# Grouping 22 mixer tiles as 2 + 6 + 6 + 8 and adding the residual by transfers in a four-layer encoder kernel

## The chip, the cores and the metric

The kernel runs on one core of a Trainium2 chip. A core has a matrix engine (TensorE, PE in the profile, with PEld for its weight loads), VectorE (DVE), ScalarE (ACT) and GpSimd (POOL), and a queue engine SyncE (SP) that here only issues transfers (DMA). Each engine takes its instructions strictly in order from its own list; semaphores hold an instruction until its inputs are there. What counts is the device time of one execution in microseconds (us); less is better.

## The reference, cut to what matters

Four layers work on x of 512 tokens by 1024 channels. Each has a token mixer (convolution, neighbourhood attention, retention, convolution) and then a gated convolutional FFN with 2816 hidden channels, that is 22 tiles of 128. The change is in the FFN alone:

```python
def rmsnorm(x, g):
    y = x * lax.rsqrt(jnp.mean(x * x, axis=-1, keepdims=True) + EPS)
    return y * g

def conv_ffn(h, w_up, dw_w, dw_b, w_down):
    u = dwconv(h @ w_up, dw_w, dw_b)          # width 3 over the tokens
    val, gate = jnp.split(u, 2, axis=-1)
    return (jax.nn.gelu(gate) * val) @ w_down

for i in range(DEPTH):
    ...
    h = rmsnorm(x, norm2_g[i])
    x = x + conv_ffn(h, ffn_w_up[i], ffn_dw_w[i], ffn_dw_b[i], ffn_w_down[i])
```

## The kernel before, in words

x lies in SBUF as eight tiles x[0..7] of 128 channels by 512 tokens, for the whole program. Every float32 operand of a product is split in a high half (a cast on ACT, "hi", "wh", "h") and a low half (source minus high half, on VectorE, "lo", "wl", "l"); mm3 (L170 to 173) makes three matmuls of them: high by high, low by high, high by low.

**FFN, up.** `up(n)` loads one tile of 1024 weights into one of two raw buffers (load_raw), splits it (split_w, L166 and L167; three buffers of each half), and makes 24 matmuls 512 wide on the eight splits of x times the norm's gain. There are 44 ups: even n the value tile n/2, odd n the gate tile. The factor 1/rms is not in these splits: `up_first` runs ups 0 and 1 together and then `stats1`, which sums the squares over channels (L211 on TensorE, L213 on VectorE) and works out rstd_col in twelve small instructions of VectorE (to L267); `stats2` spreads it over the partitions (L218 on TensorE, an ACT copy) into rstd_bc after up S2 = 2 (4 in layer 1). `mid(j)` then takes value and gate tile j: times rstd_bc (L309), the width-3 convolution (one ACT, two VectorE instructions, L312 to 316), gelu, and their product.

**FFN, down.** The 22 mixer tiles are taken as ten pairs and two left over (tiles 20 and 21). A pair is a 2 by 2 block matrix F (two tiles by two halves of the 512 tokens), and so are the weights of a macro i (output tiles 2i and 2i+1, a11, a12, a21, a22). Seven products of sums of blocks (as in Strassen's and Winograd's scheme) replace eight: mid forms the sums of F on GpSimd (L333 to L337) and splits seven blocks into Hh and Hl; `weights(i, q)` brings the raw blocks, forms s1 = a21 + a22 and s3 = a21 + a11 by accumulating transfers on GpSimd's queue (L388, L389), s2 and sg by additions on VectorE, and splits all of them. `prod` makes 3 matmuls 256 wide for each pair of the group.

The pairs come in three groups, PARTS = (0,4), (4,7), (7,10). A group's `down` runs as soon as its mids are done: the first at j = 8, the second at j = 14, the final one after all ups. In a down, each macro i works in two banks of PSUM: xc collects a11, s2, s3; v collects a22 and s1, and later sg and a12. After s2 a copy s12 of xc's states is taken and x[2i+1] is added to it on GpSimd (L464); after s3, ACT takes xc negated (L471), VectorE makes u2 = -xc - v (L473), and GpSimd adds that to x[2i] (L476). The `tail` of a macro (sg and a12 into v, then x[2i+1] = v + s12, L448) is written behind the next macro's s2. In the final group `remainder` does the two left-over tiles 512 wide for each macro, and `after(k)` prepares x[k] for the next stage: casts and low halves (L238, L241) and squares.

**What sets the order.** The code is written in one order, and a list scheduler (schedule_with_timeline_sim, in the kernel function) interleaves it by its own costs, subject to buffers and data; the result is a fixed list for each engine. `tc.issue_after(ins)` keeps an instruction behind another one. The weights of the downs in before have no such gate, so loads and splits for which a buffer is free may be placed far ahead.

## Time and profile before

| | us |
|---|---|
| median of three timed runs (2601.73 to 2607.19) | 2601.84 |
| the profiled execution, its own time | 2609.96 |
| its span in the profile | 2608.2 |
| mean granted TensorE clock of it | 0.99 |

The FFN stages begin at 211.6, 845.4, 1654.6 and 2233.6 us of the trace and last some 380 us each. The page lists busy time by engine, then what waited for what. In a row of waits the columns are: the waiting engine, its tile and line, what it waited for; then total us, times, longest us. In a window's row they are: us of the window, and for each engine the busy us with the number of instructions; then the granted clock of TensorE (1.00 is full speed), the share of the DMA engines and GB/s. In a timeline row: start in us, duration, engine, line, operation, output and inputs with their shapes, and in brackets the idle time before it and what ended it.

### The profile page before, as it was taken

Reading aid. Unit: us, or ns where it says so; the run is one execution under the profiler, and the core shown is the slowest. Engines: PE = TensorE matmul, PEld = TensorE weight load, DVE = VectorE, ACT = ScalarE, POOL = GpSimd, SP = SyncE. Lnnn points to the kernel's source line nnn. Section 1 sums busy time; section 2 is a strip of 40 time slices with the busy share of each in tenths; the row PEclk is TensorE's granted clock in tenths of the full one; section 3 lists DMA queues with packets and bytes.
Section 4 is the critical chain, followed back from the end, with each engine's and each line's share of the span. In section 5 each row is a group of like instructions: output and inputs, shape, how many; then the busy total and the mean of one; then the engine's idle time right before and its main releaser. Section 6 shows DMA issues by size and latency. Waiting matters only on the chain.

```text
span 2608.2 us, 38020 instructions
## 1 busy us (share of the span) xinstructions
PE 2544.1 (98%) x14788; PEld 2176.2 (83%) x14788; DVE 1933.9 (74%) x2980; ACT 1185.0 (45%) x1695; POOL 649.7 (25%) x649
## 2 busy tenths in 40 slices
PE   9999999989999999998999999999999999999998
PEld 7887898879998788887888888789888887789887
DVE  7976867777877887787666565687777787686777
ACT  5454444455556444444332323444444445444443
POOL 1215132234421332313000000313232221223322
PEclk9999999999999999999999999999999999999999
DMA  6726354433233544533222221535343572435443
GB/s 238 229 78 192 97 137 110 117 89 99 86 92 93 135 112 118 134 86 97 89 73 73 86 76 65 142 94 138 93 130 100 169 224 80 138 95 138 108 121 86
DMA packets 110006, 303.53 MB, mean 116 GB/s; under 512 B 14033, under 2 KB 37201, under 8 KB 109825
## 3 DMA queue, kind: packets, MB, share of 16 engines
q1 hardware_dynamic: 89136, 266.82, 33.5%
q0 software_dynamic: 19392, 31.56, 6.9%
q10 hardware_dynamic: 1296, 2.72, 0.3%
q8 instruction: 116, 1.90, 0.3%
q14 instruction: 66, 0.53, 0.1%
HBM read 291.64 MB, written 5.63 MB: 114 GB/s over the span
## 4 chain that ended last, share of the span: by engine, by line
PE 72%; DVE 9%; DMA 5%; issue 2%; ACT 2%; POOL 1%; DVEq 0%; SPq 0%; POOLq 0%; ACTq 0%
PE ps L171 20%; PE ps L173 20%; PE ps L172 20%; DVE wl L167 3%; PE ps L176 3%; PE ps L178 3%; PE ps L177 3%; DMA wt<-in_f_down 3%; DMA wr<-in_f_down 2%; ACT wh L166 1%; DVE t L314 1%; DVE t L316 1%; DVE Hl L345 1%; DVE xl L241 1%; PE ps L628 1%
## 5 line engine op out<-in xcount | busy, mean ns | idle before, releaser
L171 PE MATMUL ps<-xh,wh 128*128 128x512 f32 x1856 | 740.5, 400 | 1.2 <-ACT wh L166 1.2
L173 PE MATMUL ps<-xh,wl 128*128 128x512 f32 x1856 | 735.3, 397 | 0.1
L172 PE MATMUL ps<-xl,wh 128*128 128x512 f32 x1856 | 735.2, 396 | 0.0
L166 ACT CAST wh<-wr 128x1024 fp32r<-128x1024 f32 (+1 forms) x362 | 372.7, 1030 | 656.4 <-PE ps L172 429.3
L167 DVE TENSOR_TENSOR wl<-wr,wh 128x1024 fp32r<-128x1024 f32 (+1 forms) x359 | 448.9, 1251 | 132.4 <-ACT wh L166 131.8
L173 PEld LDWEIGHTS ps<-xh,wl 128*128 128x128 f32 x1856 | 350.4, 189 | 85.9 <-DVE wl L167 0.5
L171 PEld LDWEIGHTS ps<-xh,wh 128*128 128x128 f32 x1856 | 350.8, 189 | 83.7 <-ACT wh L166 2.8
L172 PEld LDWEIGHTS ps<-xl,wh 128*128 128x128 f32 x1856 | 350.7, 189 | 82.9 <-DVE xl L241 0.4
L173 PE MATMUL ps<-Hh,wl 128*128 128x256 f32 x640 | 176.7, 285 | 10.6 <-DVE wl L167 10.6
L172 PE MATMUL ps<-Hl,wh 128*128 128x256 f32 x640 | 180.4, 284 | 2.1 <-DVE Hl L345 1.5
L171 PE MATMUL ps<-Hh,wh 128*128 128x256 f32 x640 | 178.0, 284 | 0.4 <-ACT wh L166 0.4
L312 ACT ACTIVATE t<-t,par 128x512 f32<-128x512 f32 x176 | 141.7, 813 | 57.7 <-DVE t L309 57.0
L176 PE MATMUL ps<-wh,xh 128*128 128x256 f32 (+1 forms) x512 | 159.1, 314 | 0.4 <-ACT qk L763 0.4
L177 PE MATMUL ps<-wl,xh 128*128 128x256 f32 (+1 forms) x512 | 159.3, 312 | 0.0
L178 PE MATMUL ps<-wh,xl 128*128 128x256 f32 (+1 forms) x512 | 159.1, 312 | 0.0
L309 DVE TENSOR_TENSOR t<-ps,rstd_bc 128x512 f32<-128x512 f32 x176 | 119.4, 686 | 51.0 <-PE ps L173 49.0
L171 PE MATMUL ps<-Hh,h 128*128 128x256 f32 x480 | 139.4, 291 | 16.2 <-DVE t L473 12.3
L316 DVE SCALAR_TENSOR_TENSOR t<-t,par,t 128x511 f32<-128x511 f32 x176 | 141.3, 807 | 3.6
L314 DVE SCALAR_TENSOR_TENSOR t<-t,par,t 128x511 f32<-128x511 f32 x176 | 138.9, 794 | 0.0
L172 PE MATMUL ps<-Hl,h 128*128 128x256 f32 x480 | 138.5, 289 | 0.0
L173 PE MATMUL ps<-Hh,l 128*128 128x256 f32 x480 | 138.4, 288 | 0.0
L259 POOL TENSOR_TENSOR sqacc<-t,sqacc 128x512 f32<-128x512 f32 x49 | 75.5, 1541 | 245.4 <-ACT t L254 244.9
(297 smaller groups left out, 5301.3 us busy)
## 6 DMA issues: line engine op xcount, KB each, us to landing
wr<-in_f_up SPq DMA_DIRECT2D x176, 512.0 KB, 3.7
wraw<-in_cdw SPq DMA_DIRECT2D x56, 608.0 KB, 4.8
wr<-in_cw_in SPq DMA_DIRECT2D x30, 512.0 KB, 4.2
wr<-in_f_down SPq DMA_DIRECT2D x32, 384.0 KB, 3.2
wr<-in_nat_qkv SPq DMA_DIRECT2D x24, 512.0 KB, 3.8
wr<-in_cw_out SPq DMA_DIRECT2D x16, 512.0 KB, 4.0
wr<-in_f_down SPq DMA_DIRECT2D x16, 512.0 KB, 3.6
wr<-in_ret_qk SPq DMA_DIRECT2D x16, 512.0 KB, 3.7
```

Of the source, the lines that this page charges most:

```text
L166: nc.scalar.copy(hi[:, :n], raw[:, :n])
L167: eng.tensor_tensor(lo[:, :n], raw[:, :n], hi[:, :n].bitcast(F32), SUB)
L171: nc.tensor.matmul(o, wh, ah, start=first, stop=False, skip_group_check=free)
L172: nc.tensor.matmul(o, wh, al, start=False, stop=False, skip_group_check=free)
L173: nc.tensor.matmul(o, wl, ah, start=False, stop=last, skip_group_check=free)
L176: nc.tensor.matmul(o, ah, wh, start=first, stop=False)
L177: nc.tensor.matmul(o, ah, wl, start=False, stop=False)
L178: nc.tensor.matmul(o, al, wh, start=False, stop=last)
L309: nc.vector.tensor_tensor(u, ps, rstd_bc, MUL)
L312: nc.scalar.activation(a, u, AF.Identity, bias=pc("fdb", l * 44 + c), scale=pt[:, w + 1:w + 2])
L314: nc.vector.scalar_tensor_tensor(a[:, 1:], u[:, :T - 1], pt[:, w:w + 1], a[:, 1:], MUL, ADD)
L316: nc.vector.scalar_tensor_tensor(a[:, :T - 1], u[:, 1:], pt[:, w + 2:w + 3], a[:, :T - 1], MUL, ADD)
```

## The change

- The left-over tiles are now 0 and 1 (REST = 2), and the pairs come in groups of 3, 3 and 4: PARTS = (0,3), (3,6), (6,10), which are 6, 6 and 8 tiles. The downs still run at j = 8, 14 and at the end. The last pair of a group enters its first macro apart (`part`), after the others.
- The left-over products run once, before the final down, from an input f_rest of their own; each of the eight results is copied by ACT and added to x[k] by an accumulating transfer.
- The sums of F are three VectorE instructions a pair; one cast and one subtraction split all seven blocks.
- `weights`: one transfer writes a21 twice, one accumulating transfer adds a11 and a22 to it (r13 holds s3 and s1, three buffers). For the first macro of a group, all transfers stand behind the last up load issued (`gate`).
- The residual: x[2i+1] is added to s12, and x[2i] to u2, by accumulating transfers of GpSimd's queue (L474, L487 of the changed file, in which lines are shifted); VectorE then makes x[2i] = u2 - v (L488) and `finish`, which was `tail`, may write v. It is written behind the next macro's s3. The last macro of the final group (`direct`) does without these transfers.
- From up SCALED = 5 (7 in layer 1) on, the splits of x hold 1/rms too: eight products on VectorE into the buffers of Hh and Hl, then new splits. For those ups L309 is gone.
- TensorE has 14788 matmuls before and after. GpSimd's additions go from 400 to 148, its transfers from 241 to 313; SyncE's go from 619 to 563.

```diff
-PARTS = ((0, 4), (4, 7), (7, 10))
-PART_COL = (0, 2048, 3584, 5120)
-REST = 20
+PARTS = ((0, 3), (3, 6), (6, 10))
+PART_COL = (0, 1536, 3072)
+REST = 2
 SLOT_H = 4
-NF = 1
 NT_FFN = 7
-NWT = 2
-NWQ = 1
-DMA_SUMS = True
+NWS = 3
+SCALED = (5, 7, 5, 5)
...
         raw = wraw.tile([P, D], F32, tag="wr", name=nm("wr"))
-        nc.sync.dma_start(raw[:, :n], src)
+        state["load"] = nc.sync.dma_start(raw[:, :n], src)
         return raw
...
                 if n == S2[l]:
                     stats2()
+                    scale_first()
+                if n == SCALED[l] - 1:
+                    scale_rest()
                 return ps
+
+            xs = []
+
+            def scale_first():
+                if SCALED[l] > 2 * FT:
+                    return
+                for tag in ("Hh0", "Hl0", "Hh1"):
+                    t = hp.tile([P, 7, 256], F32, tag=tag, name=nm("xs")).rearrange("p a b -> p (a b)")
+                    xs.extend(t[:, i * T:(i + 1) * T] for i in range(3))
+                for k in range(KD):
+                    nc.vector.scalar_tensor_tensor(
+                        xs[k], x[k], pc("n2g", l * 8 + k), rstd_bc, MUL, MUL)
+
+            def scale_rest():
+                for k in range(KD):
+                    split(xs[k], xhi[k], xlo[k])
...
+                for (ps, c, n) in ((pv, j, 2 * j), (pg, j + FT, 2 * j + 1)):
+                    u = ps
+                    if n < SCALED[l]:
+                        u = t512()
+                        nc.vector.tensor_tensor(u, ps, rstd_bc, MUL)
                     w = COLS["fdw"] + (l * 44 + c) * FC
...
+                    yield
...
+                if j < REST:
...
+                p = (j - REST) // 2
...
-                gp = nc.gpsimd.tensor_tensor
...
-                    gp(F[:, 4, :], F[:, 1, :], F[:, 0, :], SUB)
...
-                gp(F[:, 7, :], F[:, 2, :], F[:, 4, :], ADD)
-                gp(F[:, 5, :], F[:, 2, :], F[:, 0, :], SUB)
-                gp(F[:, 6, :], F[:, 7, :], F[:, 3, :], SUB)
...
+                nc.vector.tensor_tensor(
+                    F[:, 4:6, :], F[:, 1:3, :], F[:, :1, :].broadcast_to([P, 2, 256]), SUB)
+                nc.vector.scalar_tensor_tensor(F[:, 0, :], F[:, 2, :], -1.0, F[:, 4, :], MUL, SUB)
+                nc.vector.scalar_tensor_tensor(F[:, 6, :], F[:, 0, :], -1.0, F[:, 3, :], MUL, SUB)
+                hi = hp.tile([P, 7, 256], F32R, tag=f"Hh{p % SLOT_H}", name=nm("Hh"))
+                lo = hp.tile([P, 7, 256], F32R, tag=f"Hl{p % SLOT_H}", name=nm("Hl"))
+                split(F, hi, lo)
+                H[p] = (hi, lo)
...
-                    nc.sync.dma_start(t[:, :n], src[:, a21])
-                    nc.sync.dma_start(s3[:, :n], src[:, a21])
-                    nc.gpsimd.dma_start(t[:, :n], src[:, a22], accum_op=ADD)
-                    nc.gpsimd.dma_start(s3[:, :n], src[:, a11], accum_op=ADD)
...
+                r13 = hp.tile([P, D], F32, tag="ws", name=nm("ws"), bufs=NWS)
+                sg = hp.tile([P, D], F32, tag="wq", name=nm("wq"))
+                with tc.issue_after(gate.ins) if gate else ExitStack():
+                    nc.sync.dma_start(
+                        r13[:, :2 * n].rearrange("p (b n) -> p b n", b=2),
+                        src[:, c + 2 * n:c + 3 * n].unsqueeze(1).broadcast_to([P, 2, n]))
+                    nc.gpsimd.dma_start(r13[:, :2 * n], src[:, c:c + 2 * n], accum_op=ADD)
+                    r1 = load_raw(src[:, c:c + 2 * n], 2 * n)
+                    nc.sync.dma_start(sg[:, n:2 * n], src[:, c + 3 * n:c + 4 * n])
                 w1 = split_w(r1, 2 * n, nc.vector)
...
+                w13 = split_w(r13, 2 * n, nc.vector)
+                r2 = hp.tile([P, T], F32, tag="w2", name=nm("w2"))
+                nc.vector.tensor_tensor(r2[:, :n], r13[:, n:2 * n], r1[:, :n], ADD)
+                h2 = hp.tile([P, T], F32R, tag="h2", name=nm("h2"))
+                l2 = hp.tile([P, T], F32R, tag="l2", name=nm("l2"))
+                split(r2[:, :n], h2[:, :n], l2[:, :n])
+                nc.vector.tensor_tensor(sg[:, :n], r2[:, :n], sg[:, n:2 * n], ADD)
...
+                split(sg[:, :2 * n], h4[:, :2 * n], l4[:, :2 * n])
...
+                return {"a11": u(w1, 0), "a22": u(w1, 1), "s3": u(w13, 0), "s1": u(w13, 1),
+                        "s2": u((h2, l2), 0), "sg": u((h4, l4), 0), "a12": u((h4, l4), 1)}
...
+            def rest_weights(c, gate):
+                with tc.issue_after(gate.ins):
+                    raw = load_raw(f_rest[l, :, c], D)
+                return split_w(raw, D, nc.vector)
+
+            def remainder(ws):
+                for c, (wh, wl) in enumerate(ws):
+                    for o in range(4):
...
+                        for k in range(REST):
+                            s = slice((o * REST + k) * P, (o * REST + k + 1) * P)
+                            mm3(ps, wh[:, s], wl[:, s], *rest[k], k == 0, k == REST - 1)
+                        t = t512()
+                        nc.scalar.copy(t, ps)
+                        nc.gpsimd.dma_start(x[c * 4 + o], t, accum_op=ADD)
...
+                def finish(i, w, v, s12):
+                    prod(v[:, :256], w["sg"], q, 2, False)
+                    prod(v[:, 256:], w["a12"], q, 3, True)
                     nc.vector.tensor_tensor(x[2 * i + 1], v, s12, ADD)
                     if final:
                         after(2 * i + 1)
...
+                    w = weights(i, q) if i else first
+                    direct = final and i == 3
...
+                    if i == 0:
+                        prod(xc, w["a11"], q, 1, True, part=range(p0, p1 - 1))
+                        prod(v[:, 256:], w["a22"], q, 6, True, part=range(p0, p1 - 1))
+                    now = range(p1 - 1, p1) if i == 0 else None
+                    prod(xc, w["a11"], q, 1, True, part=now)
                     nc.scalar.copy(s12[:, 256:], xc)
-                    prod(v[:, 256:], w["a22"], q, 5, True)
-                    prod(v[:, :256], w["s1"], q, 3, True)
-                    prod(xc, w["s2"], q, 6, False)
+                    prod(v[:, 256:], w["a22"], q, 6, True, part=now)
+                    prod(xc, w["s2"], q, 0, False)
                     nc.scalar.copy(s12[:, :256], xc)
-                    nc.gpsimd.tensor_tensor(s12, x[2 * i + 1], s12, ADD)
+                    if direct:
+                        nc.vector.tensor_tensor(s12, x[2 * i + 1], s12, ADD)
+                    else:
+                        nc.gpsimd.dma_start(s12, x[2 * i + 1], accum_op=ADD)
+                    prod(v[:, :256], w["s1"], q, 4, True)
+                    prod(xc, w["s3"], q, 5, False)
+                    u2 = t512()
+                    u2h, vh, xh2 = (t.rearrange("p (h t) -> p h t", h=2) for t in (u2, v, x[2 * i]))
+                    if direct:
+                        nc.scalar.activation(u2[:, :256], xc, AF.Copy, scale=-1.0)
+                        nc.vector.tensor_tensor(x[2 * i], x[2 * i], v, SUB)
+                        nc.vector.tensor_tensor(
+                            xh2, xh2, u2h[:, :1, :].broadcast_to([P, 2, 256]), ADD)
+                    else:
+                        nc.scalar.activation(
+                            u2h, xc.unsqueeze(1).broadcast_to([P, 2, 256]), AF.Copy, scale=-1.0)
+                        nc.gpsimd.dma_start(u2, x[2 * i], accum_op=ADD)
+                        nc.vector.tensor_tensor(x[2 * i], u2, v, SUB)
+                    if final:
+                        after(2 * i)
...
+                        finish(*prev)
...
+                    next(pieces, None)
+                for _ in pieces:
+                    pass
...
+                finish(*prev)
...
+            starts = {REST + 2 * p1: q for q, (_, p1) in enumerate(PARTS[:-1])}
             for j in range(1, FT):
                 ups_of(j)
+                w0 = weights(0, starts[j], state["load"]) if j in starts else None
...
+                if w0:
+                    done += 1
+                    down(starts[j], w0, mid(j, ups[2 * j], ups[2 * j + 1]), lambda: ups_of(j + 1))
+            gate = state["load"]
+            ws = [rest_weights(c, gate) for c in range(2)]
+            w0 = weights(0, last, gate)
             mids(FT)
-            down(len(PARTS) - 1, w0)
+            remainder(ws)
+            down(last, w0)
...
+        units = [fd[:, REST + 2 * p0 + par:REST + 2 * p1:2, :, o] for p0, p1 in PARTS
                  for o, par in ((2 * i + 1, 0), (2 * i, 1), (2 * i, 0), (2 * i + 1, 1))]
-        units += [fd[:, REST:, :, o] for o in (2 * i, 2 * i + 1)]
...
+    frest = fd[:, :REST].transpose(0, 2, 3, 1, 4).reshape(4, P, 2, 8 * P)
```

Where the instructions stand. First VectorE at the start of the FFN of layer 0, from the last low half of the tokens (xl of x[7]) on; sm is the column sum. Before:

```order
L241 SCALAR_TENSOR_TENSOR xl_102<-x_86,png,xh_94 128x512
L182 TENSOR_TENSOR l_5233<-r_5231,h_5232 128x512
L213 TENSOR_REDUCE sm_2555<-ps_2480 128x4
L167 TENSOR_TENSOR wl_2620<-wr_2617,wh_2619 128x1024
L265 TENSOR_SCALAR sm_2557<-sm_2555 128x4
L403 TENSOR_TENSOR l_3257<-ws_3240,h_3256 128x512
L167 TENSOR_TENSOR wl_2667<-wr_2664,wh_2666 128x1024
```

The same place in the change:

```order
L239 SCALAR_TENSOR_TENSOR xl_102<-x_86,png,xh_94 128x512
L211 TENSOR_REDUCE sm_2555<-ps_2480 128x4
L165 TENSOR_TENSOR wl_2631<-wr_2628,wh_2630 128x1024
L263 TENSOR_SCALAR sm_2557<-sm_2555 128x4
L165 TENSOR_TENSOR wl_2680<-wr_2677,wh_2679 128x1024
L184 TENSOR_SCALAR sm_2559<-sm_2557 128x4
```

The splits of the left-over tiles' weights (l from r) and of s3 (l from ws) have left this place; eleven small instructions and the copy to rstd_col follow in both.

Then TensorE late in the final group of layer 0. Before, the end of the last macro's s3 product (into its xc, the first three rows) and its tail (sg into its v):

```order
L171 MATMUL ps_5613<-Hh_5117,h_5598 128x256
L172 MATMUL ps_5613<-Hl_5118,h_5598 128x256
L173 MATMUL ps_5613<-Hh_5117,l_5599 128x256
L171 MATMUL ps_5614<-Hh_4791,h_5603 128x256
L172 MATMUL ps_5614<-Hl_4792,h_5603 128x256
L173 MATMUL ps_5614<-Hh_4791,l_5604 128x256
```

In the change, the end of s3 of macro 2 (its weights are wh, wl of r13 now) and macro 2's finish:

```order
L169 MATMUL ps_5380<-Hh_5066,wh_5365 128x256
L170 MATMUL ps_5380<-Hl_5067,wh_5365 128x256
L171 MATMUL ps_5380<-Hh_5066,wl_5366 128x256
L169 MATMUL ps_5381<-Hh_4634,h_5376 128x256
L170 MATMUL ps_5381<-Hl_4635,h_5376 128x256
L171 MATMUL ps_5381<-Hh_4634,l_5377 128x256
```

The place at which a product into v follows the same macro's s3 with nothing between has moved from macro 3 to macro 2. In the change, between s3 and finish, stand matmuls that take 9.28 us for macro 0 and 5.00 us for macro 1 at the rates of the trace of before (0.119 us for a 256-wide one); in the first and second downs 7.02, 9.60, 9.29 and 11.57 us for macros 0 to 3.

Last, GpSimd's queue in the first down of layer 0. Before, with a step of the next pair's sums among it:

```order
L388 DMA wt_3478<-in_f_down 128x512
L464 TENSOR_TENSOR t_3283<-x_80,t_3283 128x512
L388 DMA wt_3602<-in_f_down 128x512
L333 TENSOR_TENSOR F_3278<-F_3278 128x256
L476 TENSOR_TENSOR x_79<-x_79,t_3349 128x512
L389 DMA ws_3603<-in_f_down 128x512
```

In the change:

```order
L402 DMA ws_3419<-in_f_down 128x768
L402 DMA ws_3522<-in_f_down 128x768
L474 DMA t_3258<-x_80 128x512
L487 DMA t_3307<-x_79 128x512
L474 DMA t_3343<-x_82 128x512
```

The additions have become transfers, and all four weight sums of the down are issued ahead of the first of them.

More of the change, by code (lines that the diff above doesn't have):

```diff
@@ L288, in ffn @@
             hp = st.enter_context(tc.tile_pool(name=nm("ffn"), bufs=1, reuse_waits=RW))
+            last = len(PARTS) - 1
             def up(n):
@@ L374, in up_first, with weights @@
                 return pss
-            def weights(i, q):
+            def weights(i, q, gate=None):
                 p0, p1 = PARTS[q]
@@ L395, in weights @@
-                sg = hp.tile([P, D], F32, tag="wq", name=nm("wq"), bufs=NWQ)
-                nc.sync.dma_start(sg[:, n:2 * n], src[:, a12])
-                w1 = split_w(r1, 2 * n, nc.vector)
-                nc.vector.tensor_tensor(t[:, n:2 * n], t[:, :n], r1[:, :n], ADD)
-                w2 = split_w(t, 2 * n, nc.vector)
-                h3 = hp.tile([P, T], F32R, tag="h3", name=nm("h3"))
-                l3 = hp.tile([P, T], F32R, tag="l3", name=nm("l3"))
-                nc.scalar.copy(h3[:, :n], s3[:, :n])
@@ L417, in weights @@
                 u = lambda w, b: (w[0][:, b * n:(b + 1) * n], w[1][:, b * n:(b + 1) * n])
-                return {"a11": u(w1, 0), "a22": u(w1, 1), "s1": u(w2, 0), "s2": u(w2, 1),
-                        "s3": u((h3, l3), 0), "sg": u((h4, l4), 0), "a12": u((h4, l4), 1), "rest": lastw}
-            def prod(o, w, q, b, start, stop=True):
+                return {"a11": u(w1, 0), "a22": u(w1, 1), "s3": u(w13, 0), "s1": u(w13, 1),
+                        "s2": u((h2, l2), 0), "sg": u((h4, l4), 0), "a12": u((h4, l4), 1)}
@@ L422, in prod @@
+            def prod(o, w, q, b, start, stop=True, part=None):
                 p0, p1 = PARTS[q]
-                for p in range(p0, p1):
+                for p in part or range(p0, p1):
                     s = slice((p - p0) * P, (p - p0 + 1) * P)
@@ L427, in prod, with down @@
                         start and p == p0, stop and p == p1 - 1, True)
-            def down(q, first=None, filler=None):
-                final = q == len(PARTS) - 1
-                def remainder(i, w, s12):
-                    for o, h in ((2 * i, 0), (2 * i + 1, 2)):
-                        ps = bank(psa)
-                        for k in range(REST, FT):
-                            s = slice((h + k - REST) * P, (h + k - REST + 1) * P)
-                            mm3(ps, w["rest"][0][:, s], w["rest"][1][:, s], *rest[k],
-                                k == REST, k == FT - 1)
-                        if h:
-                            nc.vector.tensor_tensor(s12, ps, s12, ADD)
-                        else:
-                            residual(o, ps)
-                            after(o)
-                def tail(i, w, v, s12):
-                    prod(v[:, :256], w["sg"], q, 1, False)
-                    prod(v[:, 256:], w["a12"], q, 2, True)
+            def rest_weights(c, gate):
[5 more added lines that the diff above has]
+                    for o in range(4):
+                        ps = bank(psa)
+                        for k in range(REST):
[4 more added lines that the diff above has]
+                        nc.gpsimd.dma_start(x[c * 4 + o], t, accum_op=ADD)
+            def down(q, first, pieces=iter(()), filler=None):
+                final = q == last
+                p0, p1 = PARTS[q]
+                def finish(i, w, v, s12):
+                    prod(v[:, :256], w["sg"], q, 2, False)
+                    prod(v[:, 256:], w["a12"], q, 3, True)
                     nc.vector.tensor_tensor(x[2 * i + 1], v, s12, ADD)
@@ L453, in down @@
                 for i in range(4):
-                    w = first if i == 0 and first else weights(i, q)
+                    w = weights(i, q) if i else first
+                    direct = final and i == 3
                     xb, v = bank(psa), bank(psa)
@@ L490, in mids @@
                 while done < upto:
-                    mid(done, ups[2 * done], ups[2 * done + 1])
+                    for _ in mid(done, ups[2 * done], ups[2 * done + 1]):
+                        pass
                     done += 1
@@ L1343, in _layout @@
         "f_down": fdown,
+        "f_rest": frest,
     }
```

65 lines of the change are left out of this document (3 added, 62 removed).

## The prediction

> **What bounds the kernel now.** I read the page first (the span, then the busy shares), then the waits of TensorE, then busy time by windows for the stretches in which those waits lie.
>
> ```profile
> span 2608.2 us, 38020 instructions
> PE 2544.1 (98%) x14788; PEld 2176.2 (83%) x14788; DVE 1933.9 (74%) x2980; ACT 1185.0 (45%) x1695; POOL 649.7 (25%) x649
> ...
> PE ps L171 <- DVE t L473: 12.3, 4, 4.2
> PE ps L173 <- DVE wl L167: 10.6, 8, 1.8
> PE ps L218 <- DVE rstd_col L267: 9.5, 3, 3.7
> PE ps L173 <- DVE l L182: 5.9, 3, 2.5
> ```
>
> TensorE is busy 98% of the span, so only its 64 us of idle time and the stretches at a lowered clock can be won; the change keeps all 14788 matmuls. A third of VectorE's work or of GpSimd's could go without moving the end. The waits say where the idle time lies: on VectorE, in few places, four or three times each, which fits four layers. The windows give the size. Columns: us of the window, PE busy, PEld, DVE, ACT, POOL busy, granted PE clock, DMA share, GB/s.
>
> ```profile
> 211.00:245.00 34.00, 30.26 (x129) 24.24 (x128) 19.25 (x35) 12.78 (x16) 21.80 (x33) 0.95 0.89 254
> 314.00:378.00 64.00, 63.90 (x439) 59.04 (x438) 45.37 (x51) 29.25 (x43) 26.46 (x23) 1.00 0.54 133
> 420.00:485.00 65.00, 63.84 (x395) 56.74 (x394) 47.93 (x57) 28.99 (x45) 25.06 (x22) 1.00 0.54 135
> 535.00:600.00 65.00, 56.30 (x366) 52.13 (x365) 48.05 (x58) 35.74 (x49) 26.74 (x19) 0.89 0.34 90
> 1048.00:1116.00 68.00, 66.19 (x405) 58.59 (x404) 49.99 (x60) 29.70 (x46) 24.91 (x22) 1.00 0.52 130
> 1165.00:1225.00 60.00, 51.32 (x326) 46.47 (x325) 43.33 (x60) 28.99 (x51) 23.89 (x17) 0.94 0.36 96
> 1654.00:1690.00 36.00, 33.08 (x140) 26.40 (x139) 21.60 (x39) 14.61 (x20) 8.69 (x8) 0.95 0.64 174
> 1860.00:1930.00 70.00, 67.47 (x411) 59.67 (x410) 52.44 (x63) 30.02 (x47) 26.27 (x23) 1.00 0.51 133
> 1978.00:2036.00 58.00, 49.69 (x321) 45.08 (x320) 42.82 (x61) 28.26 (x50) 24.06 (x17) 0.94 0.39 104
> 2233.00:2270.00 37.00, 33.52 (x135) 26.80 (x136) 21.23 (x38) 14.05 (x19) 7.54 (x7) 0.91 0.62 164
> 2440.00:2505.00 65.00, 63.87 (x396) 56.74 (x395) 47.75 (x58) 29.23 (x45) 24.23 (x21) 1.00 0.54 135
> 2556.00:2608.00 52.00, 45.50 (x315) 41.52 (x314) 32.90 (x45) 16.66 (x31) 12.58 (x10) 1.00 0.33 89
> ```
>
> I count a window's loss as idle time plus (1 - clock) times its length. **Starts** of the FFN in layers 0, 2, 3 (211, 1654, 2233): 3.74 + 1.70 = 5.4, 2.92 + 1.80 = 4.7, 3.48 + 3.33 = 6.8, together 16.9 us. **Final groups** of layers 0 to 2 (535, 1165, 1978): 8.70 + 7.15, 8.68 + 3.60 and 8.31 + 3.48, together 39.9; that of layer 3 (2556) 6.5, the end of the program among it. **Second downs** (420, 1048, 1860, 2440): 1.16 + 1.81 + 2.53 + 1.13 = 6.6; the first down shown (314) 0.1. The rest is dense and has nothing to give.
>
> **The change, part by part. 1: the starts.** VectorE and then TensorE at the start in layer 0:
>
> ```profile
> 223.50 0.69 DVE L182 TENSOR_TENSOR l<-r,h 128x512 fp32r<-128x512 f32 x1 [8.64 <-ACT h L181]
> 224.11 0.68 DVE L213 TENSOR_REDUCE sm<-ps 128x4 f32<-128x512 f32 x1
> 226.59 0.69 DVE L403 TENSOR_TENSOR l<-ws,h 128x512 fp32r<-128x512 f32 x1 [0.59 <-ACT h L402]
> 232.80 0.16 DVE L267 COPY rstd_col<-sm 128x4 f32<-128x4 f32 x1
> ...
> 228.88 0.40 PE L173 MATMUL ps<-xh,wl 128*128 128x512 f32 x1
> 233.02 1.11 PE L218 MATMUL ps<-ident,rstd_col 128*128 128x128 f32 x4 [3.74 <-DVE rstd_col L267]
> ```
>
> The column-sum reduce (L213) that starts the chain to the inverse norm stands on VectorE behind a split of weights (l<-r) that are needed some 300 us later and wait 8.64 us for ACT, itself waiting for their load; a second such split (L403) stands inside the chain. TensorE then waits 3.74 us for rstd_col. The change gates those weights behind the last up load, and in its order both rows are gone from this place: reduce, wl, scalar, wl, eleven small ones, copy. Worked from these rows: reduce at 223.3 to 224.0, two wl of 1.25 and twelve small ones near 0.2 put the copy at about 229, where TensorE runs out at 229.2. So the wait is 0 to 0.5 instead of 3.74, and the low clock behind it goes. Layers 2 and 3 have the same two rows at the same places; there I leave 0.9 us in layer 3 that a wait for x (L697) takes today. Saved: 16.9 less about 2.4 = **14.5 us**, bounds 9 (the low clock stays) and 16. The scaling of the tokens, 8 multiplications and 8 subtractions on VectorE (0.7 each) and 8 casts on ACT, comes only after this point. Behind the broadcast of rstd_col VectorE has, from about 231.5, the eight multiplications, two wl or rstd products of up to 1.25 and the first subtraction: 231.5 + 5.8 + 1.9 + 0.7, near 240. Up number 5, the first to use the scaled halves, starts after two whole ups (24 matmuls of twice 0.119, the 256-wide step below, 5.7 each) behind 229.2, near 241. So it is hidden with about 1 us of cover at the first half and more at the later ones, and I cost it at 0, bounds 0 to 3 a layer. In return 154 multiplications by rstd (L309) go, from an engine with room.
>
> **2: the sums on GpSimd.** Groups of ups and first downs lose 0.1 us; the 160 sums of F ran beside that. Moving them to VectorE, in three instructions a pair, is 0 as long as VectorE, 45.37 busy of 64 in the window 314:378, keeps its room; it gives back its rstd products.
>
> **3: the residual through transfers.** This is what may cost. In before, x[2i] was added on GpSimd, and nothing on TensorE waited for it. Now ACT writes u2 from PSUM, GpSimd's queue adds x to it by a transfer, VectorE subtracts v, and only then may TensorE write v again (sg and a12 of that macro). No transfer of this kind, 256 KB from SBUF to SBUF with an addition, is in the trace. Nearest rows (KB, median us from issue to landing) and the two ends around it:
>
> ```profile
> wt<-in_f_down POOLq DMA_DIRECT2D x16, 256.0 KB, 4.9
> ws<-in_f_down POOLq DMA_DIRECT2D x16, 256.0 KB, 5.7
> vs<-va POOLq DMA_DIRECT2D x8, 384.0 KB, 5.2
> xf<-u POOLq DMA_DIRECT2D x112, 34.0 KB, 3.9
> ...
> L1033 ACT ACTIVATE t<-ps,rstd_col 128x512 f32<-128x512 f32 x16 | 11.0, 689 | 2.0 <-PE ps L178 1.3
> L473 DVE TENSOR_TENSOR t<-sn,ps 128x512 f32<-128x512 f32 x48 | 32.6, 679 | 0.0
> ```
>
> The first two add from HBM, ws right behind wt in the queue; the last two copy inside SBUF, and the straight line through them gives 4.7 at 256 KB. I take 4.8, near the wt row, with ends 3.9 and 5.7. Chain from the last s3 matmul to v free: most of a cast that is ahead of u2 on ACT (0.95), u2 0.69, landing, subtraction 0.68, some 0.1 of semaphores: **2.4 + landing = 7.2 us**.
>
> A 256-wide matmul costs 0.119 us (starts below, 594.61 and 594.73). In the first and second downs 59 of them, 7.02 us, stand between s3 of macro 0 and its finish, and 9.3 or more for the other macros: 0.2 us of waiting a down. I add 0.6 a down for the up that fills the gap and shares weight buffers with the last macro, in all 8 x 0.8 = 6.4, against 6.6 and a few tenths today: **0**. Ends: at a landing of 3.9 these are 5, at 5.7 they are 8 x 1.7 = 14, so -2 to +7.
>
> In the final group of layers 0 to 2 the distances are 9.28, 5.00 and 0.00 us, and macro 3 goes without the transfer. So macro 1 waits 2.2, macro 2 the full 7.2, and 1.2 more falls to splits that VectorE makes late. What a wait like that draws after it, today's rows show:
>
> ```profile
> 588.77 0.58 PE L171 MATMUL ps<-Hh,h 128*128 128x256 f32 x1 [4.17 <-DVE t L473]
> 589.15 0.41 PE L172 MATMUL ps<-Hl,h 128*128 128x256 f32 x1
> 589.36 0.41 PE L173 MATMUL ps<-Hh,l 128*128 128x256 f32 x1
> ...
> 594.61 0.28 PE L177 MATMUL ps<-wl,xh 128*128 128x256 f32 x1
> 594.73 0.28 PE L178 MATMUL ps<-wh,xl 128*128 128x256 f32 x1
> ```
>
> After 4.17 us of idling the starts lie 0.21 apart for some 24 matmuls, 24 x 0.09 = 2.2 us. Sum: 2.2 + 7.2 + 1.2 + 2.2 = 12.8 in layers 1 and 2; in layer 0 about 3 more, since the permuted casts and squares of the next stage stand ahead on ACT: 15.8. Together 41.4 against 39.9 today. Today's waits for L473 and L182 do go (macro 3 no longer needs s3, and the remainder comes first), but the wait for the transfer takes their place. Layer 3, with no next stage on ACT: +1.5. **Final groups: +3**, ends -2 (landing 3.9: macros 1 and 2 gain 0.9 each in three layers) and +10 (5.7, plus half a microsecond a layer for a full queue). One more us I count for layer 0, where the last x comes late for the next stage.
>
> The Trainium skill, "DMA: Bandwidth & Descriptors", section "Anatomy of one DMA — SWDGE (gpsimd) path", gives 2.0 us plus bytes over 436 GB/s, an estimate of 2.6 us for 256 KB. The rows above are 2 us slower than that, and the sum goes by them.
>
> **Sum.** -14.5 + 0 + 0 + 3 + 1 = -10.5 us. The profiled execution took 2609.96 (span 2608.2), so it becomes 2599.5; its 8.1 us above the median of the timed runs, 2601.84, I leave out: **2591 us**.
>
> **Rivals.** (a) *Transfers land late*, slower. Place: finish of macro 0 in every down and of macros 1 and 2 in the finals. Above 4.8 us each further us costs 8 in the downs and about 2 x 3 in the finals, 14 in all; the 10.5 are gone at a landing of 5.6, and it is slower by 5 us at 5.9. For it: ws, the second of two in that queue, has 5.7, and s12 goes into the same queue ahead of u2. Against it: s12 is issued about 2 us earlier, and the windows of the downs have a DMA share of 0.54. At 6.5 it gives 2591 + 24 = 2615. The skill's same page, section "SWDGE vs HWDGE vs iDMA", says that the descriptor rings of this path are SBUF state out of which VectorE can lock GpSimd; that speaks for (a), and no row here shows it by itself. Chance 0.17.
>
> (b) *The gain is eaten up*: starts better by only 9 and finals worse by 7, or a new wait at the starts behind the scaling (3 a layer). 2597 to 2606, chance 0.2.
>
> (c) *Transfers land quickly*. The 3.9 us of the xf row would then come from its small pieces and not from a part that every transfer pays. At 2.6 us, macro 1 waits 0 and macro 2 5.0, so 4.4 less in three layers and 1.6 in the downs: 2591 - 15 = 2576. That is the case in which the skill's formula, above, holds. All four rows speak against it; chance 0.1.
>
> (d) *The change doesn't do what it says at the starts*: rstd_col is late for another reason, such as the second wl waiting for its load, and half of the 14.5 stays: 2598. Held within (b).
>
> **How the numbers follow.** My forecast, 2584 to 2597, has 0.53. Range: from the quick landing, 2575, to the corner of all bad ends (-9 + 7 + 10 + 1, 2611) or (a) at a landing near 6.1, 2610; it leaves out some 0.1 on each side. A measurement of this kernel tells about 0.2%, 5 us, from no change: faster is below 2596.6. That holds for the forecast (0.5 of its 0.53) and (c), and a little of (b): 0.63. Same takes most of (b) and the near edge of (a), 0.21; slower 0.16.
>
> **What would show it.** Right: at 225 to 235 us the wait for rstd_col is under 1 us in layers 0, 2 and 3, and no split of weights of the down stands there. In the final groups TensorE waits for the subtraction from u2 once about 7 us and once about 2 in each of layers 0 to 2, and L473's wait is gone. The s12 and u2 transfers show a median of 4.5 to 5.2 us. In the downs, TensorE's wait at the finish of macro 0 is under 1 us. Wrong: landings of 6 or more, with waits of 1 to 3 us eight times over; or a stage start that still waits over 2 us; or a wait for the scaled low halves at up number 5.

## The result, and the profile after

The changed kernel takes 2635.83 us (median of 4 runs, 2632.34 to 2640.98), the kernel before 2602.40 on the same chip: ratio 1.0126, interval 1.0105 to 1.0147. The forecast was 2591, between 2575 and 2610: faster was expected, slower came. The profiled execution of the change has a span of 2634.7 us, 26.5 more than before.

The page of the changed kernel, then its waits of TensorE, in the columns shown before:

```profile
span 2634.7 us, 37842 instructions
PE 2548.7 (97%) x14788; PEld 2176.6 (83%) x14788; DVE 1839.4 (70%) x2934; ACT 1210.3 (46%) x1711; POOL 407.4 (15%) x469
...
PE ps L169 <- DVE x L488: 28.7, 6, 8.8
PE ps L169 <- ACT wh L164: 20.6, 16, 2.7
PE ps L169 <- ACT t L470: 8.7, 7, 2.4
PE ps L170 <- DVE Hl L180: 4.8, 7, 1.2
```

VectorE is busy 94 us less than before and GpSimd 242, and that gains nothing. The waits for L473, for rstd_col and for the left-over weights are gone; in their place stand x = u2 - v (L488), all six in the final groups, and sixteen waits for a cast of weights (L164). The windows of the changed kernel that answer to those of before (a start, a first down, a final group, the starts of layers 2 and 3, the last group):

```profile
207.00:241.00 34.00, 34.00 (x152) 27.34 (x151) 22.65 (x42) 14.22 (x20) 16.43 (x27) 1.00 0.59 181
308.00:412.00 104.00, 100.44 (x543) 85.95 (x542) 68.05 (x88) 45.07 (x62) 10.49 (x12) 0.98 0.54 134
526.00:600.00 74.00, 60.46 (x417) 56.76 (x416) 47.13 (x51) 41.95 (x54) 20.57 (x20) 0.91 0.61 136
1673.00:1709.00 36.00, 36.00 (x160) 29.01 (x159) 24.91 (x45) 14.23 (x20) 2.58 (x2) 1.00 0.22 74
2259.00:2296.00 37.00, 36.93 (x163) 29.76 (x164) 25.29 (x45) 14.11 (x21) 1.77 (x1) 1.00 0.25 74
2574.00:2634.00 60.00, 54.37 (x386) 50.81 (x384) 33.51 (x40) 24.62 (x37) 13.24 (x15) 0.97 0.68 154
```

The starts are now full at full clock. TensorE is idle for 3.6 us of the window of the first down (before, for 0.1 us of the 64 shown), and for 13.5 us of the final group's, at a clock of 0.91.

The groups differ in size between the kernels, so I compare losses in another way: each FFN is cut at the first matmul on Hh and at the last up, and from the length of each piece 0.2312 us for each 512-wide and 0.1183 for each 256-wide matmul (the steady steps) are taken off. What is left is the loss, low clock included; sums over four layers from one trace each, us. The medians were measured in four batches, in which the kernel before took 2602.40 (before, changed), 2599.84 (e1 to e4), 2596.97 (e5 to e8) and 2597.11 (e9 to e12), so times of different batches are compared by their ratios to it.

| kernel | starts | downs one and two | final groups | median, us |
|---|---|---|---|---|
| before | 22.4 | 19.9 | 43.9 | 2602.40 |
| changed | 5.3 | 50.6 | 58.0 | 2635.83 |
| e1 before with the gate | 5.3 | 75.6 | 67.0 | 2668.26 |
| e2 third raw buffer | 5.3 | 16.1 | 52.0 | 2600.84 |
| e3 u2 added on GpSimd | 5.3 | 19.4 | 37.6 | 2588.93 |
| e4 u2 without transfer | 5.3 | 21.7 | 21.1 | 2577.84 |
| e5 e4 and e2 | 5.3 | 15.7 | 22.4 | 2572.95 |
| e6 issue of a load held | 5.3 | 48.4 | 54.7 | 2630.79 (one run) |
| e7 last pair not apart | 5.3 | 41.8 | 51.8 | 2623.13 (one run) |
| e8 without scaling | 5.3 | 19.2 | 59.7 | 2607.65 (one run) |
| e9 sums on GpSimd | 5.3 | 63.5 | 87.8 | 2680.79 (one run) |
| e10 a load held | 5.3 | 60.0 | 54.3 | 2643.14 (one run) |
| e11 e5 and e7 | 5.3 | 15.7 | 23.9 | 2575.45 |
| e12 e5 and e8 | 5.3 | 14.2 | 25.8 | 2571.83 |

From before to the change: starts -17.1, downs +30.7, final groups +14.1; the two stages that follow layers 0 and 2 are 2.3 and 1.3 longer; the first mixer, which the change doesn't touch, was 4.9 shorter in this execution. Together 26.4, the 26.5 of the spans. Of the 30.7 in the downs, 18.5 are waits of TensorE (7.4 before, 25.9 now); the rest is slower matmuls.

**Where a down waits.** The first down of layer 0 in the changed kernel, by engines: the u2 transfer of macro 1 on GpSimd's queue, a load of SyncE, VectorE, that engine's next load, ACT, TensorE.

```profile
330.55 0.88 POOL L487 DMA_DIRECT2D t<-x  x1 [3.25 <-ACT t L485]
331.04 0.33 SPq L155 DMA_DIRECT2D wr<-in_f_up  x1
336.64 0.69 DVE L488 TENSOR_TENSOR x<-t,ps 128x512 f32<-128x512 f32 x1 [2.78 <-DMA t<-x]
337.25 0.69 DVE L352 TENSOR_TENSOR F<-t,t 128x512 f32<-128x512 f32 x1
337.85 0.55 DVE L412 TENSOR_TENSOR wq<-w,wq 128x384 f32<-128x384 f32 x1
338.44 0.56 DVE L408 TENSOR_TENSOR w<-ws,wr 128x384 f32<-128x384 f32 x1
339.02 0.33 SPq L155 DMA_DIRECT2D wr<-in_f_up  x1
343.64 1.04 ACT L164 CAST wh<-wr 128x1024 fp32r<-128x1024 f32 x1 [3.14 <-DMA wr<-in_f_up]
344.74 0.51 PE L169 MATMUL ps<-xh,wh 128*128 128x512 f32 x1 [2.36 <-ACT wh L164]
```

VectorE idles 2.78 us at L488 for the transfer, which takes 6.1 us to land. Queued behind it is L408, which forms s2 of macro 3 and is the last reader of one of the two raw weight buffers. Only then (339.02) does the load of up 20 go out, its cast waits 3.14 us, and TensorE stands 2.36 us. TensorE's list has two matmuls of up 20 ahead of the last 22 of up 19, so it can't go on with those. Each of the eight downs has this wait once, 2.0 to 2.7 us, 18.2 in all. Waits for the last pair's splits (Hh, Hl), up to 1.2 us, stand at the starts of the downs.

**Where a final group waits.** Layer 1, macro 2, from the cast on ACT to the finish:

```profile
1220.14 1.04 ACT L164 CAST wh<-wr 128x1024 fp32r<-128x1024 f32 x1 [1.51 <-PE ps L170]
1221.10 0.59 ACT L485 ACTIVATE t<-ps 128x512 f32<-128x512 f32 x1
1221.98 0.87 POOL L487 DMA_DIRECT2D t<-x  x1 [3.30 <-ACT t L485]
1222.47 0.33 SPq L155 DMA_DIRECT2D wr<-in_ret_qk  x1
1227.97 0.69 DVE L488 TENSOR_TENSOR x<-t,ps 128x512 f32<-128x512 f32 x1 [4.05 <-DMA t<-x]
1228.71 0.58 PE L169 MATMUL ps<-Hh,h 128*128 128x256 f32 x1 [8.39 <-DVE x L488]
1229.09 0.41 PE L170 MATMUL ps<-Hl,h 128*128 128x256 f32 x1
1229.31 0.41 PE L171 MATMUL ps<-Hh,l 128*128 128x256 f32 x1
```

This is the chain that the prediction wrote down, with a landing of 5.9 instead of 4.8: again a load is issued 0.5 us behind the transfer. Behind the wait the matmuls start 0.21 us apart instead of 0.118.

### The profile page after: what moved, and what is told of

Same layout as the page of the kernel before. It is cut to its first block, busy times and chain, and to the rows that moved or that the text cites. A ratio compares the mean times of both kernels' runs of the same rounds, so it can differ in the third digit from the quotient of the medians.

```text
span 2634.7 us, 37842 instructions
## 1 busy us (share of the span) xinstructions
PE 2548.7 (97%) x14788; PEld 2176.6 (83%) x14788; DVE 1839.4 (70%) x2934; ACT 1210.3 (46%) x1711; POOL 407.4 (15%) x469
## 4 chain that ended last, share of the span: by engine, by line
PE 81%; DMA 7%; DVE 6%; ACT 3%; issue 2%; POOL 0%; DVEq 0%; SPq 0%; ACTq 0%; POOLq 0%
PE ps L171 22%; PE ps L169 22%; PE ps L170 22%; PE ps L175 3%; PE ps L176 3%; PE ps L174 3%; DMA t<-x 2%; DMA ws<-in_f_down 2%; DMA wr<-in_f_down 1%; DVE wl L165 1%; DMA wr<-in_f_up 1%; PE ps L648 1%; PE ps L647 1%; PE ps L646 1%; ACT wh L164 1%
## 5 line engine op out<-in xcount | busy, mean ns | idle before, releaser
L169 PE MATMUL ps<-xh,wh 128*128 128x512 f32 x1856 | 734.0, 397 | 19.2 <-ACT wh L164 19.1
L164 ACT CAST wh<-wr 128x1024 fp32r<-128x1024 f32 (+1 forms) x370 | 380.9, 1031 | 689.2 <-PE ps L170 418.9
L402 POOL DMA_DIRECT2D ws<-in_f_down x48 | 42.3, 882 | 777.1 <-DMA ws<-in_f_down 744.4
L169 PEld LDWEIGHTS ps<-Hh,wh 128*128 128x128 f32 x640 | 121.0, 191 | 15.1 <-ACT t L470 9.4
L170 PEld LDWEIGHTS ps<-Hl,wh 128*128 128x128 f32 x640 | 122.3, 191 | 7.2 <-DVE Hl L180 6.2
L169 PEld LDWEIGHTS ps<-Hh,h 128*128 128x128 f32 x480 | 95.2, 198 | 34.4 <-DVE x L488 26.5
L171 PEld LDWEIGHTS ps<-Hh,wl 128*128 128x128 f32 x640 | 119.0, 192 | 3.0 <-DVE wl L165 2.1
```

The source lines that it names most:

```text
L164: nc.scalar.copy(hi[:, :n], raw[:, :n])
L169: nc.tensor.matmul(o, wh, ah, start=first, stop=False, skip_group_check=free)
L170: nc.tensor.matmul(o, wh, al, start=False, stop=False, skip_group_check=free)
L171: nc.tensor.matmul(o, wl, ah, start=False, stop=last, skip_group_check=free)
L402: nc.gpsimd.dma_start(r13[:, :2 * n], src[:, c:c + 2 * n], accum_op=ADD)
```

## The experiments

**e1, the gate alone, on the kernel before.** The transfers of `weights` moved under a gate:

```diff
-            def weights(i, q):
+            def weights(i, q, gate=None):
...
+                with tc.issue_after(gate.ins) if gate else ExitStack():
+                    r1 = load_raw(src[:, c:c + 2 * n], 2 * n)
...
-                    w = first if i == 0 and first else weights(i, q)
+                    w = first if i == 0 and first else weights(i, q, gate)
...
-                        w0 = weights(0, q)
+                        w0 = weights(0, q, state["load"])
```

> The kernel before, with one part of the change alone: the transfers of a group's weights (for the later macros too) stand behind the last up load or the first weight load of the group. Theory (each part of the change acts by itself): the starts of the FFN lose 22.4 us in before and 5.3 in the change, so this gives 17 us: 2585, with no wait for rstd_col above 1 us. Rival (the gate is what makes the downs slow, because the weights come late): the starts gain the same 17, but the eight downs lose 2 to 4 us each more, and the time is 2600 to 2617.

Measured 2668.26 us (ratio 1.026, 1.023 to 1.029). The starts give the 17.1 us, alone and in full. The downs lose 55.7 more, the rival's direction and more than its price, and the final groups 23.1. This gate is wider than that of the change, which leaves the later macros' transfers free; what the wider part adds was not measured. TensorE's waits in e1:

```profile
PE ps L171 <- ACT Hh L342: 38.3, 8, 7.2
PE ps L173 <- DVE wl L167: 13.0, 13, 3.1
```

Each of the eight downs waits once for the last pair's Hh, 2.7 to 7.2 us, at its start. The gate brings a down's weights when the last pair's sums (VectorE, GpSimd, ACT) are due as well. My reading is that the gain at the starts was bought with cover that the hoisted weights had given; no run tests that reading by itself.

**e2, three raw weight buffers in the changed kernel.**

```diff
-NRAW = 2
+NRAW = 3
```

> The changed kernel with three raw weight buffers instead of two. Theory (VectorE stands at x = u2 - v until the transfer has landed; r2, which is the last reader of a raw buffer, is queued behind it; so the load of the second filler up goes out late): the eight waits of TensorE for a cast wh of 2.0 to 2.7 us at that up go below 0.5, and the low clock behind them (1.5 us each) goes too; the loss of the downs falls from 50.6 us to about 20, the final groups stay at 58, time 2605 to 2610. Rivals (the sums of F on VectorE, or the gated weights, make the downs slow): the waits stay at 2 us or more and the time at 2630 to 2640.

Measured 2600.84 us (ratio to before 1.0005, 0.9996 to 1.0014; the change had 1.0126, so some 31 us less). The time is below the 2605 to 2610 expected; the downs fall from 50.6 to 16.1. The waits that lead its list; those for wh are no longer among them:

```profile
PE ps L169 <- DVE x L488: 27.0, 6, 8.7
PE ps L169 <- ACT t L470: 8.9, 6, 2.9
PE ps L623 <- DVE t L617: 3.8, 2, 1.9
PE ps L169 <- ACT Hh L179: 2.0, 1, 2.0
```

TensorE's list has up 20's two matmuls at the same place, and u2 of macro 1 still lands in 6.0 us (first down). So the buffer that r2 holds is what turned VectorE's wait into TensorE's. The sums on VectorE and the gated weights are still there, so they don't explain the 50.6. Of the 34.5 us, 18 are the eight waits, 12 the slower matmuls behind waits, and the rest mostly waits for Hh and Hl. The final groups fall by 6.0, where I had expected no change.

**e3 and e4, the transfer of x[2i] replaced.** e3 adds x to u2 with an instruction of GpSimd; e4 takes for every macro the way that the final macro 3 has.

```diff
-                        nc.gpsimd.dma_start(u2, x[2 * i], accum_op=ADD)
+                        nc.gpsimd.tensor_tensor(u2, x[2 * i], u2, ADD)
```

```diff
                     u2h, vh, xh2 = (t.rearrange("p (h t) -> p h t", h=2) for t in (u2, v, x[2 * i]))
-                    if direct:
+                    if True:
```

> The changed kernel with x[2i] added to u2 by an instruction of GpSimd (1.4 to 1.8 us) instead of an accumulating transfer (3.3 us alone, 6 beside a 512 KB load). Theory (the transfer's landing is what TensorE and VectorE wait for): x = u2 - v comes 2 to 4 us earlier; the downs lose about 20 us instead of 50.6, the wait at the finish of macro 2 in the final groups falls from 8.4-8.8 to about 4.5 in three layers, time 2590 to 2600. Rivals (sums of F on VectorE, gated weights): downs and time as in the changed kernel, 2625 to 2640.

> The changed kernel with the way of the final macro 3 for every macro: x[2i] - v and then + u2 on VectorE, no transfer for x[2i] (s12 keeps its transfer). Theory: v is read without waiting for s3, so nothing waits at finish; the downs lose about 20 us instead of 50.6, the final groups lose the 8.4-8.8 us wait and about 2 of low clock three times, 2560 to 2580. Rivals (VectorE is crowded by the sums of F and two more instructions a macro): downs lose 50 or more, time 2610 to 2640.

e3: 2588.93 us (0.9957, 0.9944 to 0.997); e4: 2577.84 (0.9918, 0.9898 to 0.9938). Both beat the kernel before; e3 comes just under its range, e4 within. Downs of 19.4 and 21.7, final groups of 37.6 and 21.1. First the waits for v in e3, then the list of e4, in which L488's and L481's are gone:

```profile
PE ps L169 <- DVE x L488: 15.9, 7, 4.7
```

```profile
PE ps L169 <- ACT t L467: 8.1, 3, 3.5
PE ps L623 <- DVE t L617: 3.8, 2, 1.9
PE ps L175 <- DVE wl L165: 3.6, 2, 3.5
PE ps L170 <- DVE Hl L180: 3.6, 6, 1.2
```

With GpSimd's instruction (1.3 to 2.1 us) the longest wait is 4.7 where the transfer makes 8.8. In e4, with no wait for v behind s3, the final groups lose 21.1 instead of 58.0, 37 us less.

**e5, e4 with the third buffer.** 

> Both cures at once: no transfer for x[2i] and three raw weight buffers. Theory (two separate waits, one for the transfer and one for the raw buffer that r2 holds): e4 still lost 21.7 us in the downs where e2 lost 16.1, and 21.1 in the final groups; here the downs lose 8 to 14 and the final groups about 20, 2566 to 2573. Rival (one cause: once nothing waits at x = u2 - v the third buffer has nothing left to give): 2575 to 2581, as e4.

2572.95 us (0.9904, 0.9884 to 0.9924), at the upper edge of what the theory gave. The downs lose 15.7, 6.0 less than in e4, where 8 to 14 was expected; the final groups stay at 22.4. The intervals of e4 and e5 overlap, and the 6.0 are a sum of one trace with both signs (layer 1 loses 3.0 more, layer 2 6.5 less). So whether the third buffer has anything left to give is not shown, and the rival is not excluded.

**e6 and e10, does a load beside it slow the transfer?** e6 asked for the load of the first filler up to be issued behind the transfer (`tc.issue_after`); e10 makes the load wait for x[2]:

```diff
+                if held:
+                    nc.vector.tensor_copy(raw[:, :1], x[2][:, :1])
+                state["load"] = nc.sync.dma_start(raw[:, :D], f_up[l, c])
```

> The changed kernel with the load of the first filler up of each down (512 KB, in the changed kernel issued 0.3 to 0.5 us after the u2 transfer of macro 1) held behind that transfer. Theory (a transfer with an addition lands in 3.3 us alone and in about 6 when a 512 KB load is issued within half a microsecond): the eight u2 transfers of macro 1 land in 3.3 to 4.3 us instead of 4.9 to 6.7; those of macro 2, beside another load, stay at 5.8 to 6.4. Rival (they are slow for another reason, such as their place in the down): all stay at 5 to 6.7. The time says little, since that up's weights come later: 2625 to 2655.

> The changed kernel with the load of the first filler up of each down really held (e6 held only its issue, which came 0.5 us behind as before): one element of the raw buffer is first copied from x[2], so that the load goes out only after x[2] = u2 - v of macro 1. Theory (a 512 KB load issued within half a microsecond of the transfer makes it land in about 6 us instead of 3.3): the eight u2 transfers of macro 1 land in 3.3 to 4.3 us. Rival (they are slow for another reason): 5 to 6.7 as before. The time says little, since that up's weights come some 5 us later: 2625 to 2665.

e6 is inconclusive: in its trace that load went out ahead of the transfer as before, and the load that comes beside macro 1's transfer is the following up's (up 19; in the changed kernel too, where up 18's goes out 9.6 us ahead of it). Its landings, 4.6 to 7.5, say nothing. In e10 no load of SyncE was issued from 1.0 us ahead of macro 1's transfers to 1.3 us behind them. All eight landings of u2 by macro of the downs, us, taken from the traces:

```
                     macro 1                                    macro 2
changed    6.1 6.7 4.9 6.1 6.1 6.5 6.3 6.0       6.4 5.8 5.9 6.2 6.3 6.0 6.1 5.9
e10        3.3 4.8 3.3 3.3 3.3 4.8 3.3 3.3       5.5 5.6 6.0 6.6 6.1 6.9 5.8 7.9
```

The macro whose neighbour was taken away lands in 3.3 in six of eight, at the same place in the down; the other one, with a load still beside it, stays at 5.5 to 7.9. That shows the load as the cause. In the two that land in 4.8, an instruction packet (queue q8 of the profile) of 1.0 and 1.2 us runs among the transfer's packets; that it delays them was not tested. One pair of rows of e10, the transfer and the subtraction that waited for it:

```profile
325.59 0.88 POOL L491 DMA_DIRECT2D t<-x  x1 [2.42 <-ACT t L489]
...
328.98 0.69 DVE L492 TENSOR_TENSOR x<-t,ps 128x512 f32<-128x512 f32 x1
```

The time, 2643.14, says little, as expected: the held up's weights come late, and the downs lose 60.0.

**e7 and e11, the last pair not apart.**

```diff
-                    if i == 0:
-                        prod(xc, w["a11"], q, 1, True, part=range(p0, p1 - 1))
-                        prod(v[:, 256:], w["a22"], q, 6, True, part=range(p0, p1 - 1))
-                    now = range(p1 - 1, p1) if i == 0 else None
+                    now = None
```

> The changed kernel without the separate entry of a group's last pair: macro 0 takes a11 of all pairs, then a22 of all. Theory (with gated weights, this entry is what hides the split of the last pair, since the kernel before with the gate waited up to 7.2 us there): the waits for Hh and Hl at the start of the downs grow from 0.6 to 1.7 us a down to 2 to 5, the loss of the downs from 50.6 to 60 to 80 us, time 2640 to 2665. Rival (the interleaving of the last mid and the order of the loads do that): no more than 4 us difference, 2630 to 2640.

> e5 (no transfer for x[2i], three raw buffers) without the separate entry of the last pair, which took 9 us off the downs in e7. Theory (the separate entry brings the products that wait for the last pair's splits ahead of those that don't): 5 to 9 us less than e5, 2564 to 2568. Rival (in e7 it was a matter of the buffers, which e5 has cured): within 3 us of e5, 2570 to 2576.

e7: 2623.13 in one run, downs 41.8. My theory is refuted, and the rival with its 4 us too: the separate entry hid nothing, the downs were better by 8.8 without it. But e11, on top of e5, gives 2575.45 (0.9916, 0.9899 to 0.9932), downs 15.7 as in e5: with the buffer cured the entry is indifferent, as the rival had it. The traces say where the 8.8 us lay: 1.9 in the waits for wh, 2.5 in those for Hh and Hl, the rest in slower matmuls. Why the entry costs this only in the change isn't shown.

**e8 and e12, without scaling the tokens.**

```diff
-SCALED = (5, 7, 5, 5)
+SCALED = (99, 99, 99, 99)
```

> The changed kernel without the scaling of the tokens: every product of the ups is multiplied by rstd on VectorE, as before. Theory (the scaling is hidden and costs or gives nothing on TensorE): starts 5.3 us of loss as now, time within 6 us of 2636. Rival (it gives VectorE room that the downs need): downs lose 60 us or more, time 2645 or more.

> e5 without the scaling of the tokens. Theory (in e8 leaving it out helped only because the scheduler then placed the filler ups otherwise; the scaling itself is hidden): with the buffer wait cured, within 4 us of e5, 2569 to 2577. Rivals: the scaling costs by itself, 2555 to 2568; or it gives VectorE room, 2578 to 2590.

e8 did what neither theory said: 2607.65 in one run, downs 19.2. In its list of TensorE up 20 no longer stands ahead of up 19's rest, and its longest wait for wh is 0.4. The load of up 20 still goes out late there (in the first down at 336.83, behind L408 at 336.24), but TensorE has up 19 to go on with. So the place of up 20 in TensorE's list is a third condition of the wait, beside the transfer and the buffer. On top of e5, where that place is harmless, leaving out the scaling gives 2571.83 (0.9899, 0.9884 to 0.9913) against 2572.95: no difference. So the scaling itself is neutral there, and in the change it did its harm by what the scheduler made of it.

**e9, the sums of F on GpSimd again**, in six instructions a pair, since the blocks now need other signs (four in before).

```diff
+                gp = nc.gpsimd.tensor_tensor
                 if j % 2 == 0:
+                    gp(F[:, 4, :], F[:, 1, :], F[:, 0, :], SUB)
+                    gp(F[:, 7, :], F[:, 0, :], F[:, 1, :], SUB)
                     return
+                gp(F[:, 5, :], F[:, 2, :], F[:, 0, :], SUB)
+                gp(F[:, 0, :], F[:, 7, :], F[:, 2, :], SUB)
+                gp(F[:, 7, :], F[:, 2, :], F[:, 3, :], SUB)
+                gp(F[:, 6, :], F[:, 7, :], F[:, 4, :], ADD)
```

> The changed kernel with the sums of F on GpSimd again (two instructions behind a pair's first tile, four behind its second). Theory (the sums on VectorE matter at one place: with gated weights nothing else fills the start of a down, and there the last pair would pass VectorE, GpSimd, ACT and VectorE, as in e1): the waits for Hh and Hl at the start of the downs grow from 0.4 to 1.7 us a down to 3 to 6, the loss of the downs from 50.6 to 65 to 85 us, time 2650 to 2670. Rival (where the sums run is indifferent, as the prediction had it): downs within 5 us of 50.6, time 2630 to 2642.

2680.79 us in one run; downs 63.5, a little under what was expected, and final groups 87.8, which I hadn't expected to move.

```profile
PE ps L169 <- ACT Hh L179: 21.8, 12, 4.1
PE ps L170 <- DVE Hl L180: 9.1, 12, 1.3
```

The waits for the pairs' splits grow from 6.0 (4.8 for Hl, 1.2 for Hh) to 30.9 us: 13.8 in the eight downs, 1.7 each and not the 3 to 6 expected, and 17.1 at the starts of the four final groups. In this kernel, with gated weights, the sums belong on VectorE.

## Why the prediction was wrong, point by point

1. **The starts** were right. 14.5 us forecast, 17.1 measured, with 1.3 of it in layer 1, which I had left out. e1 shows that the gate alone does it. What the step missed is the price of a gate: I looked for what is late next at the start only, not at the place where the weights now arrive. e9 shows that a gate costs less with the sums on VectorE.

2. **The sums of F** were costed at 0 for the dense stretches, where that held. At the start of a group the choice matters: on GpSimd (e9) the downs lose 12.9 us more and the final groups 29.8.

3. **The downs: the step that failed.** It read: 7.02 us of matmuls between s3 and finish of macro 0, "9.3 or more for the other macros: 0.2 us of waiting a down", and 0.6 for the weight buffers, so 0 in all with ends of -2 and +7. Measured +30.7. TensorE never waits for v in the downs, so the arithmetic on finish was right. But a wait was added on VectorE, and the step didn't ask what is queued behind it there: L408, the raw buffer, a load, a cast. e2 takes away the buffer wait, e3 and e4 the transfer and e8 the place of up 20 in TensorE's list, and each takes 29 to 35 of the 50.6 us off. The 0.6 a down for shared weight buffers named the right resource, with a price that was worked out from no row; the wait there measured 2.0 to 2.7, with slower matmuls behind it.

4. **The final groups**: the mechanism was right, two sizes not: +3 forecast with ends of -2 and +10, +14.1 measured. The larger miss is the low clock. In layers 0 to 2 the sum had 2.2 us a layer behind the waits, 6.6 in all; beside the waits these groups lose 5.6, 5.6 and 3.7, or 14.9, about as much as before (14.3), and the clock of their windows is 0.91, 0.88 and 0.91. The other is the waits: the sum had 2.2 + 7.2 + 1.2 a layer and about 3 more in layer 0, 34.8 in all, and TensorE waits 13.5, 12.3 and 11.9, or 37.7. The landing at macro 2 is 5.9 to 6.3 where 4.8 was taken, and its waits are 8.4 to 8.8 instead of 7.2. Macro 1 waits 0.9 to 1.3 instead of 2.2 (its transfer is alone, 3.3). The s2 copy on ACT (L470), behind a split that waits for VectorE, costs 2.2 to 2.4 instead of 1.2.

5. **The scaling** at 0 was right as a cost of its own (e12), but it changed the scheduler's list (e8). **The next stages**: 1 us forecast, 3.6 measured.

6. **The rivals.** (a), transfers that land late, had the sign and a chance of 0.17, but not the place: macro 0 of a down lands in 3.3 to 4.1 us, and no finish in a down waits. The sign of being wrong (landings of about 6, waits of 1 to 3 us eight times over) did come, at the cast of up 20. Nor was it (a)'s reason: at macro 1 of a down s12 is issued about 4 us ahead of u2 and has landed by then; what is beside u2 is a load of SyncE. The median landing of all 88 transfers is 4.0 us, below the 4.8 that I took:

```profile
t<-x POOLq DMA_DIRECT2D x88, 256.0 KB, 4.0
```

The 44 u2 transfers alone have a median of 4.7, almost my figure, and the step was wrong all the same. A median was the wrong thing to compare: the landings fall in groups, and the slow group lies where it is waited for. A line through two median rows could not show that. The estimate of 2.6 us from the Trainium skill, "DMA: Bandwidth & Descriptors", section "Anatomy of one DMA — SWDGE (gpsimd) path", is nearer to the 3.3 of a transfer alone than my 4.8 was, and far from the 6 beside a load.

## What to carry to other kernels

When an instruction gets a new wait, list what stands behind it on its own engine, and follow each down to the buffer it frees, the load that wants the buffer and the engine that wants the load, and what that engine's list could do meanwhile; here the downs, where that chain lies, became 30.7 us longer, the final groups, whose waits I had priced, 14.1. Price a transfer by what else is issued in the same microsecond, not by its median. Gating work that is in the way at one place moves it to another, where it has to be paid for again: here a gate alone (e1) made the kernel 2.6% slower, while kernels that hold a gate and the right company (e5, e12) are about 1% faster than before.

## What the runs showed of the hardware

The u2 transfers (256 KB from SBUF to SBUF with an addition, on GpSimd's queue) land in 3.3 us with no load beside them, in about 4.0 when a 512 KB load of SyncE is issued 0.8 us behind it (7 of 8 in the changed kernel), and in 5.8 to 6.7 when that load comes 0.3 to 0.5 us behind (18 of 18). That of macro 2 in the final group of layer 3, with no next stage to load for, took 3.3. The seven traces that hold these transfers agree: of the 308, 66 have one such load 0.2 to 0.5 us behind and land in 5.5 to 7.5; 60 have none from 3 us ahead to 2.5 us behind, and 58 of them land in 3.3 to 3.9 (the others are the two of 4.8 in e10).

The DMA packets of the changed kernel's trace show why half a microsecond decides. Alone, a transfer's first packet moves 1.44 us after its issue and its last ends at 2.97. A load's first packet moves about 1 us after the load's issue. With the load 0.3 to 0.5 us behind, the load's packets begin at 1.2 to 1.7 us of the transfer's time, and the transfer's first packet comes only at 3.2 to 3.8 (15 of 15 in the downs). With the load 0.8 us behind, the transfer keeps its 1.44, and it is the load whose first packet is put off, to 3.5 us (7 of 8; in the eighth an instruction packet of 1.4 us runs among them, and the transfer lands in 6.4). So one of the two goes first and the other stands behind it. At half a microsecond both would begin together, and there it was the load that went first each time; what decides that, no run here shows.
